# A two-layer diffusion trunk: last norm's statistics on ScalarE, five-operation norm chain, half-step loads reordered, MLP gate rows by TensorE

## The chip, the cores and the metric

The kernel runs on one core of a Trainium2 chip. The metric is the device time of one execution in microseconds (us). Engines are named as the profile names them: PE is TensorE (PEld its weight loads), DVE is VectorE, ACT is ScalarE, POOL is GpSimd, and SP issues every DMA of this kernel, in the order in which they were recorded.

## The reference, cut to what matters

Two transformer-like layers run over 128 context tokens and 512 latent tokens, 1024 wide. Each layer has a mixer and an MLP, and each of these two ends in a layer norm:

```python
def _block(x, mod, mixer, g, b, w1, w2):
    sh1, sc1, gt1, sh2, sc2, gt2 = jnp.split(mod, 6, axis=-1)
    mix, aux = mixer(x * (1 + sc1) + sh1)
    x = _layer_norm(ALPHA * x + gt1 * mix, g[0], b[0])
    hf = x * (1 + sc2) + sh2
    ff = jnp.square(jax.nn.relu(hf @ w1)) @ w2
    x = _layer_norm(ALPHA * x + gt2 * ff, g[1], b[1])
    return x, aux
```

The six rows of `mod` (kinds 0 to 5: shift, scale and gate of the mixer, then of the MLP) come from `silu(cond) @ w_mod[l] + b_mod[l]`, with one condition vector for the context and one for the latents. `w_mod` is 1024 x 6144 for each layer, so it is a matrix product with two rows and 24 MB of weights per layer. Kind 5 is the gate of the MLP. Layer 0's mixer (the even one) is retention beside differential attention; layer 1's (the odd one) is windowed attention beside gated linear attention (GLA). All is float32 in and out.

## The kernel before, in words

The tokens are five tiles of 128 (tile 0 the context). The width is two halves of 512. Every large product is taken in three matmuls of split numbers: a value is cast to a high part (`whi`, `ghi`, `hh`) and the remainder (`wlo`, `glo`, `hl`) is a DVE subtraction; `whi` is an ACT cast. Weights come in units of 512 KB (`wraw`), which are split before PE can use them.

**What sets the order.** All DVE, ACT and POOL operations are recorded by one helper (`Timed.run`, L380), all loads by `load` (L454), matmuls by `mm` (L470), transposes at L485; so most rows of the profile carry these lines, and the tile names tell them apart. A planner (class `Order`, L131) keeps a model of the engines' times while the kernel is being written and interleaves chains of work; the resulting order is fixed. PE executes in that order, and so do the other queues: an engine never passes a waiting instruction.

**The modulation rows** are computed in three ways. The shift and scale of layer 0's mixer are needed at once, and so are computed on PE at the start (`matvec`, in two halves of eight k-steps; tiles `mod` and `wmod`). Kinds 2, 3 and 4 of layer 0 are done by `ModPE` (L634): for each of 6 pieces, two batches of 16 matmuls (`modp<-wmodp,cs`) in the even mixer, a piece every `MOD_PE` = 38 us of the planner's time. Kind 5 of layer 0 and all six of layer 1 are done by `ModChunk` (L574) without PE except for a closing sum over partitions (`modps`): eight steps per chunk of 512 columns, each a 256 KB load, a scaled sum into `moda` for the context column and one for the latent column. In each step with k > 0 POOL does a TENSOR_SCALAR on `wmod` and a TENSOR_TENSOR `moda<-moda,wmod`; the other sum is on ACT (`modp`) and POOL (`moda<-moda,modp`) for layer 0, and one DVE SCALAR_TENSOR_TENSOR (`moda<-wmod,cs,moda`) for layer 1. The `background` function issues a step every `MOD_SPACE` = 3.6 us of planner time from the first MLP on, 14 chunks of 8 steps in all, kind 5 of layer 0 first, and holds them during norms.

**The MLP** has 8 groups g of 512 hidden columns: `ff` (first product), `relu`, square into `ghi` and `glo`, then `fps` (second product). Layer 0's last group is where the next layer's columns are also formed (`A`, `B`).

**The norm** (`norm`, L939) takes, per token tile, two BN_STATS and a BN_AGGR on DVE, a square root on ACT, and six DVE operations on 128x1: `ve`, reciprocal `r`, `q`, `q`, `r`, `nmr`. In the last norm, tiles 0 to 2 (and half of tile 3) are scaled by ACT and multiplied and added by POOL (`x<-x,lnrow`), the rest on DVE.

**The start** (from L1098) loads the first half's 8 k-steps of `w_mod`, four weight units and the inputs xT, forms the first half of the first modulation, modulates the five tiles' first half (`modulated`, two ACT and two POOL operations per tile on `h`, then a cast `h0h` and a remainder `h0l` on DVE) and interleaves early products (`early`) with the second half's matrix-vector steps.

Of the kernel before, what the change touches and what calls it, by code (L numbers as in the profile page):

```python
# [9 lines left out]
F32 = mybir.dt.float32  # L10
F32R = mybir.dt.float32r
I32 = mybir.dt.int32
AF = mybir.ActivationFunctionType
# [5 lines left out]
P = 128  # L19
# [3 lines left out]
KT = 8  # L23
# [13 lines left out]
NSPL = 5  # L37
DEC0, DEC = 0.0, 2.0
MOD_SPACE = 3.6
MOD_PE = 38.0  # L40
LO_POOL = 0
DRS = False
UPD = 30.0
WD = 3
WS = 2
# [362 lines left out]
def trunk_kernel(ctx: ExitStack, tc: tile.TileContext, io: dict, layers: int = 2, stop: str = ""):  # L408
# [3 lines left out]
    const = ctx.enter_context(tc.tile_pool(name="const", bufs=1))  # L412
    hpool = ctx.enter_context(tc.tile_pool(name="hpool", bufs=4))
    gpool = ctx.enter_context(tc.tile_pool(name="gpool", bufs=NSLOT))
    mtmp = ctx.enter_context(tc.tile_pool(name="mtmp", bufs=1))
    mraw = ctx.enter_context(tc.tile_pool(name="mraw", bufs=MRAW))
    wraw = ctx.enter_context(tc.tile_pool(name="wraw", bufs=NRAW))
    wspl = ctx.enter_context(tc.tile_pool(name="wspl", bufs=NSPL))
# [7 lines left out]
    def nm(s):  # L426
        uid[0] += 1
        return f"{s}_{uid[0]}"
# [6 lines left out]
    def sm(s, shape):  # L435
        tag = "s" + "x".join(map(str, shape[1:]))
        t = small.tile(shape, F32, tag=tag, name=nm(s))
        order.reuse(tag, NSMALL, t)
        return t
# [134 lines left out]
    class ModChunk:  # L574
# [10 lines left out]
        def step(self, k):  # L585
            raw = self.raw.pop(k)
            if k == KT - 2:
                self.b = slot("brow")
                src = io["b_mod"][self.l, 512 * self.c:512 * self.c + 512].rearrange("(e n) -> e n", e=2)
                for e in range(2):  # L590
                    load(self.b[64 * e:64 * e + 64, :256], src[e].partition_broadcast(64))
            if k == 0:
                self.A = [slot("moda"), slot("moda")]
            a0, a1 = (a[:, :512] for a in self.A)
            if k == 0:
                act.activation(a0, raw, AF.Copy, scale=cs[:, k, 0:1])
                pool.tensor_scalar(a1, raw, cs[:, k, 1:2], 0.0, op0=ALU.mult, op1=ALU.add)
            else:
                if self.l == 0:
                    tmp = mtmp.tile([P, 512], F32, tag="modp", name=nm("modp"))  # L600
                    order.reuse("modp", 1, tmp)
                    act.activation(tmp, raw, AF.Copy, scale=cs[:, k, 0:1])
                    pool.tensor_tensor(a0, a0, tmp, op=ALU.add)
                else:
                    stt(a0, raw, cs[:, k, 0:1], a0, op0=ALU.mult, op1=ALU.add)
                pool.tensor_scalar(raw, raw, cs[:, k, 1:2], 0.0, op0=ALU.mult, op1=ALU.add)
                pool.tensor_tensor(a1, a1, raw, op=ALU.add)
            if k == KT - 1:
                order.spawn(self.finish())
# [93 lines left out]
                add_piece((l, "2", g, n), [Unit(io["w_2"][l, g, n, u], 2, 512) for u in range(2)])  # L703
    pos = [0, 0, 0]
    mod_steps = []
    for l, kinds in ((0, (5,)), (1, range(6))):
        if l < layers:
            for c in kinds:
                for a in range(2):
                    chunk = ModChunk(l, 2 * c + a)  # L710
                    mod_steps += [(chunk, k) for k in range(KT)]
    mod_left = [0.0, len(mod_steps)]
    mod_hold = [False]
    split_hold = [False]

    mod_pe = [ModPE(2 * c + a) for c in (2, 3, 4) for a in range(2)]

    def load_unit():
        units[pos[2]].load()
        pos[2] += 1  # L720

    def split_unit():
        if pos[0] == pos[2]:
            load_unit()
        units[pos[0]].split()
        pos[0] += 1
# [212 lines left out]
    def norm(t, rows, ft, A, B, final, key, xd=None):  # L939

        cuts = [(0, 0, 512), (1, 0, 512)] if t < NT - 1 else [(0, 0, 256), (0, 256, 512), (1, 0, 256), (1, 256, 512)]
        st = sm("bn", [P, 4, 6])[:, :len(cuts), :]
        mv = sm("mv", [P, 2])
        for i, (a, c0, c1) in enumerate(cuts):
            dve.bn_stats(st[:, i, :], X[t][a][:, c0:c1])
        dve.bn_aggr(mv, st)
        if DRS:
            ve = sm("ve", [P, 1])
            dve.tensor_scalar(ve, mv[:, 1:2], EPS, None, op0=ALU.add)
            r = rsqrt(ve, [P, 1])  # L950
        else:
            ve = sm("ve", [P, 1])
            sq = sm("sq", [P, 1])
            act.activation(sq, mv[:, 1:2], AF.Sqrt, bias=eps_t)
            dve.tensor_scalar(ve, mv[:, 1:2], EPS, None, op0=ALU.add)
            r = sm("r", [P, 1])
            q = sm("q", [P, 1])
            dve.reciprocal(r, sq)
            vec_tt(q, r, r, op=ALU.mult)
            stt(q, q, -0.5, ve, op0=ALU.mult, op1=ALU.mult)  # L960
            stt(r, q, 1.5, r, op0=ALU.add, op1=ALU.mult)
        nmr = sm("nmr", [P, 1])
        stt(nmr, mv[:, 0:1], -1.0, r, op0=ALU.mult, op1=ALU.mult)
        if not final:
            xn = X[t]
            for a in range(2):
# [136 lines left out]
    load_unit()  # L1103
    xt = load_x(0)
    load_unit()
    load_unit()
    ps = acc("mod0")
    for k in range(KT):
        matvec(0, k, ps)
    row = mod_row(ps)  # L1110
    split_unit()
    load_unit()
    dls = slot("dl")
    bc_row(dls[:, :256], io["diff_lam"])
    bc_row(sk, io["swa_sink"])
    for k in range(KT):
        load_mod0(1, k)
    xt1 = load_x(1)
    load(cst[:, C_RC:], io["consts"][:, C_RC:])
    mod_cols(0, row)  # L1120
    order.give()
# [2 lines left out]
    split_unit()  # L1124
    for t in range(1, NT):
        modulated(0, xt, t)
    split_unit()
    split_unit()
    lam(dls)
    ps = acc("mod0")  # L1130
    for k in range(KT):
        for t in range(NT):
# [8 lines left out]
    load_unit()  # L1141
    for t in TURN:
        modulated(1, xt1, t)
    start.close()
    order.give()
    order.fifo = False
# [1017 lines left out]
```

## Time and profile before

| what | value |
|---|---|
| median of 3 runs | 1669.2 us (1667.19 to 1670.53) |
| the profiled execution | 1671.51 us, of which the span is 1669.7 us |
| mean granted PE clock | 0.979 of full speed |
| PE busy | 1579.6 us (95%) |
| DVE busy | 1046.0 us (63%) |
| ACT busy | 619.9 us (37%) |
| POOL busy | 582.2 us (35%) |
| DMA | 177.87 MB, mean 107 GB/s |

PE is busy for 95% of the span, so the kernel's time is PE's work plus the 90 us in which PE is idle or ends before the rest. Where PE waits, the trace names the instruction on another engine that released it. A time at the start of a row counts from the start of the span.

### The profile page before, as it was taken

The page shows a single profiled execution, that of the slowest core. Times are in us where ns is not written, and L with a number is a line of the kernel's source. Part 1 is how long each engine was busy: PE and PEld are TensorE (multiplying, and loading weights), DVE is VectorE, ACT ScalarE, POOL GpSimd, SP SyncE. Part 2 cuts the span into 40 slices and gives each one's busy share as a digit, 9 for nine tenths or more (in the row PEclk, how much of TensorE's full clock was granted, in tenths as well). Part 3 has the DMA queues.
Part 4 walks back from the last instruction along what each step waited for, and adds up shares of the span by engine and source line. Part 5 has one row for each costly group of instructions (what it writes and reads, how often), then busy time and mean ns, then how long its engine had stood idle before and what let it go on. Part 6 is the DMA issues. An engine that isn't in the chain of part 4 may idle for free. (4 is left out here: it accounts for less than half of the span.)

```text
span 1669.7 us, 28365 instructions
## 1 busy us (share of the span) xinstructions
PE 1579.6 (95%) x11233; PEld 1431.6 (86%) x11233; DVE 1046.0 (63%) x1963; ACT 619.9 (37%) x1294; POOL 582.2 (35%) x493
## 2 busy tenths in 40 slices
PE   7999999999999999999898898979999999999995
PEld 4998999998989988998787887869989989998994
DVE  3777762685377667767877787777833334444458
ACT  2555443336433312221265454553543222222221
POOL 1110000111896687678557445340200110011215
PEclk9999999999999999999998998989999999999998
DMA  9523333332444444543424210014222221223121
GB/s 345 185 86 93 97 112 105 130 115 64 137 148 151 146 146 152 171 148 106 146 80 137 73 36 28 27 56 141 76 72 68 76 89 60 72 79 115 55 76 63
DMA packets 89764, 177.87 MB, mean 107 GB/s; under 512 B 23576, under 2 KB 30752, under 8 KB 89632
## 3 DMA queue, kind: packets, MB, share of 16 engines
q1 hardware_dynamic: 89632, 176.07, 32.6%
q8 instruction: 88, 1.44, 0.3%
q14 instruction: 44, 0.36, 0.1%
HBM read 169.53 MB, written 6.50 MB: 105 GB/s over the span
## 5 line engine op out<-in xcount | busy, mean ns | idle before, releaser
L470 PE MATMUL ff<-hh,whi 128*128 128x320 f32 (+2 forms) x960 | 297.1, 309 | 0.0
L470 PE MATMUL ff<-hh,wlo 128*128 128x320 f32 (+2 forms) x960 | 296.4, 309 | 0.1
L470 PE MATMUL ff<-hl,whi 128*128 128x320 f32 (+2 forms) x960 | 296.3, 309 | 0.0
L380 DVE TENSOR_TENSOR wlo<-wraw,whi 128x1024 fp32r<-128x1024 f32 (+1 forms) x183 | 243.3, 1334 | 80.4 <-ACT whi L380 80.2
L380 ACT CAST whi<-wraw 128x1024 fp32r<-128x1024 f32 (+1 forms) x183 | 189.5, 1045 | 278.8 <-PE fps L470 244.7
L470 PE MATMUL fps<-whi,glo 128*128 128x512 f32 (+1 forms) x648 | 254.3, 393 | 5.1 <-DVE glo L380 5.1
L470 PE MATMUL fps<-wlo,ghi 128*128 128x512 f32 (+1 forms) x648 | 253.7, 391 | 2.3 <-DVE wlo L380 2.3
L470 PE MATMUL fps<-whi,ghi 128*128 128x512 f32 (+1 forms) x648 | 254.9, 393 | 0.0
L380 POOL TENSOR_TENSOR x<-x,lnrow 128x512 f32<-128x512 f32 (+1 forms) x76 | 105.9, 1402 | 351.6 <-DVE y L380 214.5
L380 DVE TENSOR_TENSOR relu<-relu 128x320 f32<-128x320 f32 (+3 forms) x100 | 70.7, 707 | 186.6 <-ACT ghi L380 185.6
L470 PEld LDWEIGHTS ff<-hh,whi 128*128 128x128 f32 x960 | 180.2, 188 | 3.1 <-issue 2.1
L470 PEld LDWEIGHTS ff<-hl,whi 128*128 128x128 f32 x960 | 180.2, 188 | 0.6
L470 PEld LDWEIGHTS ff<-hh,wlo 128*128 128x128 f32 x960 | 180.2, 188 | 0.3 <-DVE wlo L380 0.3
L380 ACT ACTIVATE relu<-ff 128x320 f32<-128x320 f32 (+3 forms) x100 | 51.4, 514 | 278.7 <-PE ff L470 276.2
L380 DVE TENSOR_TENSOR y<-fps,y 128x512 f32<-128x512 f32 x120 | 82.7, 689 | 111.6 <-PE fps L470 111.5
L470 PEld LDWEIGHTS fps<-whi,glo 128*128 128x128 f32 x648 | 122.1, 188 | 33.2 <-DVE glo L380 5.5
L380 POOL TENSOR_TENSOR moda<-moda,wmod 128x512 f32<-128x512 f32 x98 | 146.0, 1490 | 6.8
L470 PEld LDWEIGHTS fps<-wlo,ghi 128*128 128x128 f32 x648 | 122.1, 188 | 30.3 <-DVE wlo L380 3.5
L470 PEld LDWEIGHTS fps<-whi,ghi 128*128 128x128 f32 x648 | 122.0, 188 | 29.0 <-issue 2.5
L380 POOL TENSOR_SCALAR wmod<-wmod,cs 128x512 f32<-128x512 f32 x98 | 112.7, 1150 | 92.8 <-DVE moda L380 81.4
L380 POOL TENSOR_TENSOR o<-o,sg 128x640 f32<-128x640 f32 x8 | 13.0, 1621 | 257.7 <-ACT o L380 257.3
L470 PE MATMUL proj<-whi,hh 128*128 128x256 f32 (+1 forms) x280 | 85.1, 304 | 12.5 <-DVE gm L380 7.6
(298 smaller groups left out, 3527.7 us busy)
## 6 DMA issues: line engine op xcount, KB each, us to landing
wraw<-in_w SPq DMA_DIRECT2D x128, 512.0 KB
wmod<-in_w_mod SPq DMA_DIRECT2D x144, 256.0 KB
wraw<-in_w_even SPq DMA_DIRECT2D x24, 512.0 KB
wmodp<-in_w_mod SPq DMA_DIRECT2D x48, 256.0 KB
wraw<-in_w_out SPq DMA_DIRECT2D x16, 512.0 KB
wraw<-in_w_odd SPq DMA_DIRECT2D x16, 512.0 KB
gate<-mrow SPq DMA_DIRECT2D x16, 256.0 KB
xT<-in_xT SPq DMA_DIRECT2D x8, 320.0 KB
```

Source lines behind the costliest of these rows:

```text
L380: i = f(*a, **k)
L470: nc.tensor.matmul(o, a, b, **kw)
```

## The change

Five edits are made together.

1. In the last norm, for tiles 0 to 2, mean and variance come from ACT: two Identity passes with an accumulator (sums, into `part`), a DVE TENSOR_SCALAR for `nmean`, two Square passes with the bias `nmean`, and two DVE TENSOR_SCALARs for `mv`. BN_STATS and BN_AGGR go there.
2. The small chain of all norms has five DVE operations (`veh`, reciprocal in place, `q`, `r`, `nmr`), four of them TENSOR_SCALARs with per-partition operands; before it was six, of which one was TENSOR_TENSOR and three SCALAR_TENSOR_TENSOR.
3. At the start, the third weight unit of four stays where it was, the fourth and the row of `diff_lam` are loaded after the second half's `w_mod` and xT. The two last unit splits move behind the second half's first modulated tile, and `lam` behind all of them.
4. Kind 5 of layer 0 leaves `ModChunk` (16 of 112 steps) and becomes two more pieces of `ModPE` (eight in all).
5. `MOD_PE` is 30 instead of 38.

```diff
-MOD_PE = 38.0
+MOD_PE = 30.0
...
             else:
-                if self.l == 0:
-                    tmp = mtmp.tile([P, 512], F32, tag="modp", name=nm("modp"))
-                    order.reuse("modp", 1, tmp)
-                    act.activation(tmp, raw, AF.Copy, scale=cs[:, k, 0:1])
-                    pool.tensor_tensor(a0, a0, tmp, op=ALU.add)
-                else:
-                    stt(a0, raw, cs[:, k, 0:1], a0, op0=ALU.mult, op1=ALU.add)
+                stt(a0, raw, cs[:, k, 0:1], a0, op0=ALU.mult, op1=ALU.add)
...
-    for l, kinds in ((0, (5,)), (1, range(6))):
-        if l < layers:
-            for c in kinds:
-                for a in range(2):
-                    chunk = ModChunk(l, 2 * c + a)
-                    mod_steps += [(chunk, k) for k in range(KT)]
+    for c in range(6 if layers > 1 else 0):
+        for a in range(2):
+            chunk = ModChunk(1, 2 * c + a)
+            mod_steps += [(chunk, k) for k in range(KT)]
...
-    mod_pe = [ModPE(2 * c + a) for c in (2, 3, 4) for a in range(2)]
+    mod_pe = [ModPE(2 * c + a) for c in (2, 3, 4, 5) for a in range(2)]
...
+        if final and t < 3:
+            junk = slot("junk")[:, :512]
+            part = sm("part", [P, 4])
+            nmean = sm("nmean", [P, 1])
+            for a in range(2):
+                act.activation(junk, X[t][a][:, :512], AF.Identity, accum_out=part[:, a:a + 1])
+            dve.tensor_scalar(nmean, part[:, 0:1], part[:, 1:2], -1.0 / D, op0=ALU.add, op1=ALU.mult)
+            for a in range(2):
+                act.activation(junk, X[t][a][:, :512], AF.Square, bias=nmean, accum_out=part[:, 2 + a:3 + a])
+            dve.tensor_scalar(mv[:, 1:2], part[:, 2:3], part[:, 3:4], 1.0 / D, op0=ALU.add, op1=ALU.mult)
+            dve.tensor_scalar(mv[:, 0:1], nmean, -1.0, None, op0=ALU.mult)
...
+        act.activation(sq, mv[:, 1:2], AF.Sqrt, bias=eps_t)
+        dve.tensor_scalar(veh, mv[:, 1:2], EPS, -0.5, op0=ALU.add, op1=ALU.mult)
+        dve.reciprocal(sq, sq)
+        dve.tensor_scalar(q, sq, sq, veh, op0=ALU.mult, op1=ALU.mult)
+        dve.tensor_scalar(r, q, 1.5, sq, op0=ALU.add, op1=ALU.mult)
+        dve.tensor_scalar(nmr, mv[:, 0:1], -1.0, r, op0=ALU.mult, op1=ALU.mult)
...
     load_unit()
     xt = load_x(0)
     load_unit()
-    load_unit()
...
     split_unit()
+    for k in range(KT):
+        load_mod0(1, k)
+    xt1 = load_x(1)
+    load_unit()
     load_unit()
     dls = slot("dl")
...
-    for k in range(KT):
-        load_mod0(1, k)
-    xt1 = load_x(1)
...
-    split_unit()
-    split_unit()
-    lam(dls)
     ps = acc("mod0")
...
     for t in TURN:
         modulated(1, xt1, t)
+        if t == TURN[0]:
+            split_unit()
+            split_unit()
+    lam(dls)
```

The order on the engines changes with this in places that the diff does not show. On DVE, at the end of layer 0's MLP (last group), before: `relu` and `glo` are the first product's results on their way to the second product, and the `moda` rows are modulation steps of layer 1.

```order
L380 TENSOR_TENSOR glo_8757<-relu_1489_8893,ghi_8756 128x640
L380 SCALAR_TENSOR_TENSOR moda_8798<-wmod_8864,cs,moda_8798 128x512
L380 TENSOR_TENSOR wlo_8934<-wraw_8728,whi_8933 128x1024
L380 TENSOR_TENSOR relu_1492_8928<-relu_1492_8928 128x320
L380 TENSOR_TENSOR glo_8759<-relu_1492_8928,ghi_8758 128x320
L380 SCALAR_TENSOR_TENSOR moda_8798<-wmod_8898,cs,moda_8798 128x512
L380 TENSOR_TENSOR brow_8732<-modps_8972,brow_8732 128x256
L380 TENSOR_TENSOR wlo_8983<-wraw_8836,whi_8982 128x1024
L380 TENSOR_TENSOR relu_1497_8967<-relu_1497_8967 128x320
L380 TENSOR_TENSOR glo_8759<-relu_1497_8967,ghi_8758 128x320
L380 SCALAR_TENSOR_TENSOR moda_8798<-wmod_8937,cs,moda_8798 128x512
```

And now, at the same place of DVE's order:

```order
L379 TENSOR_TENSOR glo_8840<-relu_1492_8963,ghi_8839 128x640
L379 TENSOR_TENSOR wlo_8999<-wraw_8813,whi_8998 128x1024
L379 TENSOR_TENSOR relu_1494_8993<-relu_1494_8993 128x320
L379 TENSOR_TENSOR glo_8842<-relu_1494_8993,ghi_8841 128x320
L379 TENSOR_TENSOR brow_8815<-modps_9032,brow_8815 128x256
L379 TENSOR_TENSOR wlo_9041<-wraw_8911,whi_9040 128x1024
L379 TENSOR_TENSOR relu_1498_9027<-relu_1498_9027 128x320
L379 TENSOR_TENSOR glo_8842<-relu_1498_9027,ghi_8841 128x320
```

All 96 remaining steps now stand 16 steps earlier among the other work, so the last of them has left DVE before these rows. On POOL, in the odd mixer, before: `x<-x,lnrow` rebuilds the trunk's tiles after the MLP's norm, and `gA` and `Eq` belong to the GLA gates.

```order
L380 TENSOR_SCALAR wmod_9910<-wmod_9910,cs 128x512
L380 TENSOR_TENSOR x_4473<-x_4473,lnrow_9062 128x512
L380 TENSOR_TENSOR moda_9907<-moda_9907,wmod_9910 128x512
L380 TENSOR_TENSOR x_4473<-x_4473,lnrow_9066 128x512
L380 TENSOR_SCALAR wmod_10003<-wmod_10003,cs 128x512
L380 TENSOR_SCALAR wmod_10035<-wmod_10035,cs 128x512
L380 TENSOR_TENSOR moda_9907<-moda_9907,wmod_10003 128x512
L380 MEMSET gA_10166 128x5
L380 TENSOR_TENSOR moda_9907<-moda_9907,wmod_10035 128x512
L380 MEMSET gA_10174 128x5
L380 TENSOR_TENSOR Eq_10192<-gA_9955 128x5x64
```

And now, up to the same `Eq`:

```order
L379 TENSOR_TENSOR x_4546<-x_4546,lnrow_9110 128x512
L379 MEMSET gA_9966 128x5
L379 MEMSET gA_9974 128x5
L379 TENSOR_TENSOR x_4546<-x_4546,lnrow_9114 128x512
L379 TENSOR_TENSOR x_4401<-x_4401,lnrow_9108 128x512
L379 TENSOR_TENSOR x_4401<-x_4401,lnrow_9112 128x512
L379 TENSOR_TENSOR x_4589<-x_4589,lnrow_9110 128x512
L379 TENSOR_TENSOR x_4589<-x_4589,lnrow_9114 128x512
L379 TENSOR_TENSOR Eq_10137<-gA_9974 128x5x64
```

No modulation step is left on POOL or DVE in the odd mixer. The last place is DVE in the last norm, before, for tile 2 and the beginning of tile 3 (`fps` is the MLP's second product, `tmp` its product with the gate):

```order
L380 BN_STATS bn_17227<-x_12915 128x6
L380 TENSOR_TENSOR tmp_17224<-fps_17211,gate_16343 128x512
L380 BN_STATS bn_17227<-x_13109 128x6
L380 TENSOR_TENSOR x_12953<-x_12953,tmp_17224 128x512
L380 BN_AGGR mv_17228<-bn_17227 128x2
L380 TENSOR_SCALAR ve_17232<-mv_17228 128x1
L380 TENSOR_TENSOR tmp_17265<-fps_17252,gate_16345 128x512
L380 RECIPROCAL r_17236<-sq_17233 128x1
L380 TENSOR_TENSOR x_13141<-x_13141,tmp_17265 128x512
L380 TENSOR_TENSOR q_17237<-r_17236 128x1
L380 SCALAR_TENSOR_TENSOR q_17237<-q_17237,ve_17232 128x1
L380 SCALAR_TENSOR_TENSOR r_17236<-q_17237,r_17236 128x1
```

And now, for the same stretch:

```order
L379 TENSOR_TENSOR tmp_17202<-fps_17189,gate_16311 128x512
L379 TENSOR_TENSOR x_12933<-x_12933,tmp_17202 128x512
L379 TENSOR_SCALAR nmean_17208<-part_17207 128x1
L379 TENSOR_TENSOR tmp_17248<-fps_17235,gate_16313 128x512
L379 TENSOR_TENSOR x_13114<-x_13114,tmp_17248 128x512
L379 TENSOR_SCALAR mv_17205<-part_17207 128x1
L379 TENSOR_SCALAR mv_17205<-nmean_17208 128x1
L379 TENSOR_SCALAR veh_17216<-mv_17205 128x1
L379 RECIPROCAL sq_17217<-sq_17217 128x1
L379 TENSOR_SCALAR q_17218<-sq_17217,veh_17216 128x1
L379 TENSOR_SCALAR r_17219<-q_17218,sq_17217 128x1
```

Two BN_STATS are gone per tile, and three 128x1 operations wait there for ACT's passes: `nmean` stands ahead of the next tile's second `tmp`, `mv` behind it.

## Rows read from the trace of the kernel before

**Rows 1.** Windows: length, PE, PEld, DVE, ACT, POOL busy, PEclk, DMA share, GB/s.
```profile
27.70:45.00 17.30, 16.73 (x143) 11.51 (x144) 5.07 (x13) 1.62 (x3) 0.71 (x1) 1.00 1.01 376
70.00:345.00 275.00, 266.39 (x2432) 255.86 (x2432) 177.39 (x524) 119.95 (x317) 11.42 (x7) 0.99 0.34 107
345.00:800.00 455.00, 451.08 (x2664) 405.27 (x2663) 307.22 (x387) 154.28 (x248) 308.65 (x234) 1.00 0.42 132
900.00:945.00 45.00, 32.85 (x282) 30.75 (x281) 39.03 (x62) 15.02 (x27) 29.99 (x32) 0.81 0.30 98
1020.00:1121.00 101.00, 81.64 (x842) 71.04 (x840) 75.63 (x196) 50.45 (x139) 46.77 (x55) 0.86 0.11 35
```

**Rows 2.** Timeline of PE, layer 0's last MLP group, then layer 1's; brackets: idle before.
```profile
811.96 0.39 PE L470 MATMUL fps<-whi,ghi 128*128 128x512 f32 x1
...
819.74 0.79 PE L470 MATMUL fps<-whi,glo 128*128 128x512 f32 x1 [5.07 <-DVE glo L380]
...
824.80 0.50 PE L470 MATMUL fps<-wlo,ghi 128*128 128x512 f32 x1 [1.28 <-DVE wlo L380]
...
1621.95 0.39 PE L470 MATMUL fps<-whi,ghi 128*128 128x512 f32 x1
...
1627.53 0.50 PE L470 MATMUL fps<-wlo,ghi 128*128 128x512 f32 x1 [1.01 <-DVE wlo L380]
```

**Rows 3.** Timeline of DVE, in the first of these waits.
```profile
812.08 1.78 DVE L380 SCALAR_TENSOR_TENSOR moda<-wmod,cs,moda 128x512 f32<-128x512 f32 x1
...
814.11 1.61 DVE L380 TENSOR_TENSOR wlo<-wraw,whi 128x1024 fp32r<-128x1024 f32 x1
```

**Rows 4.** Timeline of PE in the odd mixer.
```profile
903.05 2.42 PE L470 MATMUL z<-glT,w 32*128 32x320 f32 x8
913.11 0.58 PE L470 MATMUL proj<-whi,hh 128*128 128x256 f32 x1 [7.64 <-DVE gm L380]
```

**Rows 5.** Timeline of DVE there: the scans of the GLA gates, two groups.
```profile
902.62 8.19 DVE L380 TENSOR_TENSOR_SCAN gA<-ones,ge 128x128 f32<-128x128 f32 x8
...
930.66 1.68 DVE L380 TENSOR_TENSOR_SCAN gA<-ones,ge 128x128 f32<-128x128 f32 x5
```

**Rows 6.** What PE waited for from 895 to 945: total, times, longest.
```profile
PE gl L470 <- DVE gST L380: 2.9, 1, 2.9
PE proj L470 <- DVE ropea L380: 1.6, 1, 1.6
```

**Rows 7.** Groups of instructions: forms, count, busy us, mean ns; layer 0's rows on PE.
```profile
L470 PE MATMUL modp<-wmodp,cs 128*32 128x128 f32 x384 | 13.0, 276 | 0.0
...
L470 PE MATMUL modps<-moda,ones 128*32 128x256 f32 x112 | 8.9, 391 | 0.0
```

**Rows 8.** Timeline of the start, on PE and DVE.
```profile
27.68 0.63 PE L470 MATMUL mod<-wmod,cs 128*32 128x256 f32 x4 [1.74 <-DMA wmod<-in_w_mod]
...
47.73 0.43 DVE L380 CAST h0h<-h 128x512 fp32r<-128x512 f32 x1 [0.36 <-POOL h L380]
...
49.30 0.48 DVE L380 CAST h0h<-h 128x512 fp32r<-128x512 f32 x1 [0.36 <-POOL h L380]
```

**Rows 9.** Timeline of the last norm on DVE and ACT.
```profile
1642.32 1.24 DVE L380 TENSOR_TENSOR q<-r 128x1 f32<-128x1 f32 x1
...
1643.98 0.16 DVE L380 SCALAR_TENSOR_TENSOR nmr<-mv,r 128x1 f32<-128x1 f32 x1
...
1651.26 0.16 DVE L380 SCALAR_TENSOR_TENSOR nmr<-mv,r 128x1 f32<-128x1 f32 x1
...
1644.18 1.52 ACT L380 ACTIVATE x<-x,nmr,r 128x512 f32<-128x512 f32 x2 [4.29 <-DVE nmr L380]
```

**Rows 10.** Groups: accumulating ACT passes, and a small DVE operation of the norms.
```profile
L380 ACT ACTIVATE sp<-ss,smx 128x512 f32<-128x512 f32 x16 | 10.9, 682 | 16.7 <-DVE smx L380 16.3 <-DVE ssum L380 0.4
...
L380 ACT ACTIVATION_READ_ACCUMULATOR sp<-ss,smx 128x1 f32 x40 | 7.9, 198 | 0.0
...
L380 DVE TENSOR_SCALAR ve<-mv 128x1 f32<-128x1 f32 x20 | 3.0, 149 | 0.2
```

More of the change, by code (lines that the diff above doesn't have):

```diff
@@ L39 @@
 MOD_SPACE = 3.6
-MOD_PE = 38.0
+MOD_PE = 30.0
 LO_POOL = 0
-DRS = False
 UPD = 30.0
@@ L414, in trunk_kernel @@
     gpool = ctx.enter_context(tc.tile_pool(name="gpool", bufs=NSLOT))
-    mtmp = ctx.enter_context(tc.tile_pool(name="mtmp", bufs=1))
     mraw = ctx.enter_context(tc.tile_pool(name="mraw", bufs=MRAW))
@@ L941, in norm @@
         cuts = [(0, 0, 512), (1, 0, 512)] if t < NT - 1 else [(0, 0, 256), (0, 256, 512), (1, 0, 256), (1, 256, 512)]
-        st = sm("bn", [P, 4, 6])[:, :len(cuts), :]
         mv = sm("mv", [P, 2])
[L944 to L950, printed above, removed]
-        else:
[L952 to L961, printed above, removed]
@@ L962, in norm @@
-        nmr = sm("nmr", [P, 1])
-        stt(nmr, mv[:, 0:1], -1.0, r, op0=ALU.mult, op1=ALU.mult)
+        if final and t < 3:
[9 more added lines that the diff above has]
+            dve.tensor_scalar(mv[:, 0:1], nmean, -1.0, None, op0=ALU.mult)
+        else:
+            st = sm("bn", [P, 4, 6])[:, :len(cuts), :]
+            for i, (a, c0, c1) in enumerate(cuts):
+                dve.bn_stats(st[:, i, :], X[t][a][:, c0:c1])
+            dve.bn_aggr(mv, st)
@@ L964, in norm @@
+        veh, sq, q, r, nmr = (sm(n, [P, 1]) for n in ("veh", "sq", "q", "r", "nmr"))
+        act.activation(sq, mv[:, 1:2], AF.Sqrt, bias=eps_t)
[4 more added lines that the diff above has]
+        dve.tensor_scalar(nmr, mv[:, 0:1], -1.0, r, op0=ALU.mult, op1=ALU.mult)
         if not final:
```

## The prediction, as put on record before the run

> **What bounds the kernel now.** I read first the busy shares by window, then PE's idle gaps and their releasers in each stretch where PE is not full, and last the other engines in those gaps. PE is the bound almost everywhere: in the even mixer it is busy for 266.4 of 275 us, in layer 0's MLP for 451.1 of 455 [rows 1]. There only PE's own work counts, and DVE or ACT work is free as long as it isn't late. PE is not full in four places. (A) In the last group of layer 0's MLP it waits 5.07 us for `glo`, then 1.28 for `wlo` [rows 2]; DVE spends that time on a modulation step of 1.78 us and a `wlo` of 1.61 [rows 3]. (B) and (C) In the odd mixer, from 900 to 945, PE is busy for 32.85 of 45 us at a mean granted clock of 0.81 [rows 1]: it waits 7.64 us for `gm` [rows 4], 2.9 for `gST` and 1.6 for `ropea` [rows 6]. At the end of that mixer, 1020 to 1121, it is busy for 81.6 of 101 us [rows 1]; the change moves nothing there. The last place is the norm after PE's last product, where DVE's chain sets the end.
>
> The sum is made against the profiled execution, 1671.5 us, which lies 2.3 us above the median of the runs, 1669.2; I apply the difference to the median. A measurement of this kernel can't tell less than about 0.2%, 3.3 us, from no change.
>
> **The start.** The fourth weight unit (512 KB) and `diff_lam`'s row (128 KB), 0.64 MB, go behind the second half's loads. From 27.7 to 45 the DMAs run at 376 GB/s with a busy share of 1.01 [rows 1], so the loads that PE waits for come 0.64 MB / 376 GB/s = 1.7 us earlier. Against it, the split of the last two units now stands behind the second half's first tile: a tile takes 49.30 - 47.73 = 1.57 us on DVE [rows 8], and PE's next early products need these splits, so they may come up to two tile-times later than if split under the DMA's wait. I take a loss of 1.4 and a net of -0.3, range -1.7 (the splits hide) to +1.5 (the gain is eaten by a wait of two tiles).
>
> **Kind 5 on PE.** All batches of ModPE have 16 matmuls, and six pieces are 12 batches: 13.0 us, so 1.08 per batch [rows 7]. Two more pieces add four batches, 4.3 us. Of the partition sums, 8 of 56 go: 8.9 x 8/56 = 1.3 us [rows 7]. Net +3.1, at full price, because PE is full in the even mixer; lower end 0, if the batches fill the 8.6 us that PE idles there, upper end +4.5, if the sums that go were already hidden. A shorter spacing (30 for 38) adds no instruction. The 1 MB per piece is small beside the DMA's share of 0.34 there.
>
> **Place A.** The 96 steps of layer 1 start 16 steps earlier, so none stands beside the last group any more; DVE was busy for only 307 of 455 us in the MLP [rows 1], and takes them there. What A is worth is read from layer 1's MLP, where the same stretch of matmuls runs with no step beside it: 1627.53 - 1621.95 = 5.58 us, against 824.80 - 811.96 = 12.84 in layer 0 [rows 2]. So -7.3; range -5 (the wait of 5.07 alone) to -8.
>
> The mechanism behind it is that DVE and POOL hold each other up: eight `gA` scans take 8.19 us beside POOL's steps, five take 1.68 when POOL is idle [rows 5], that is 1.02 against 0.34 each. The Trainium skill says in "SBUF — State Buffer", section "SBUF: two separate sides", that a DVE operation with two SBUF inputs, or one in a 2-port mode, and a GpSimd operation exclude each other for a whole instruction; on the scans these rows agree with it. It speaks against one part of this change: by that rule the TENSOR_SCALARs of the new small chain would be held as the old operations were, if they count as 2-port ones, and the last norm would gain 1 us less, a sum of -17.2. The trace's `ve` TENSOR_SCALAR is 0.149 us on average of 20 [rows 10], with POOL busy beside many of them, so I don't follow it there.
>
> **Places B and C.** No step stands on DVE or POOL in the odd mixer now, so `gm` follows `z` without the scans' 8.19 us being stretched (at 0.34 they would be 2.7), and POOL's `Eq` no longer stands behind steps. Idle time of PE there is 45 - 32.85 = 12.15 us [rows 1]. The clock takes more: 0.81 over the stretch costs at most 32.85 x 0.19 = 6.2 us, an estimate that counts idle time too; I take 5. That is 17.2 us. What is late next: PE, no longer held, comes earlier to the matmuls that need the gates' chain (z, `gm`, `ge`, scan, `Eq`, `gST`), which keeps its own length. I leave one wait of the kind of C in place, 2.9 + 1.6 = 4.5 us [rows 6]. So -12.7; range -17.2 (all goes) to 0 (PE finds the same waits elsewhere).
>
> **The small chain.** One 128x1 operation of 0.15 us [rows 10] fewer in 20 tiles, and one of `q` that was held 1.24 us in the last norm [rows 9] is now a TENSOR_SCALAR. In the three norms before the last, only the last tile's is on the way to PE: -0.5, range -2 to 0.
>
> **The last norm.** Per tile, DVE loses two BN_STATS and a held `q`, but three operations wait for ACT. ACT's passes are nearest to `sp`, 0.68 + 0.20 = 0.88 us each [rows 10]; four are 3.5, the scaling of the tile 1.5 [rows 9], and with the root, the small operations between (some eight at 0.15 to 0.2) and hand-overs I come to 7.0 to 7.4 us per tile in a ring ACT - DVE - ACT. Before, the tiles' `nmr` are 1651.26 - 1643.98 = 7.28 apart [rows 9]. So tile 3 begins as late as before; after it, two held small operations fall away, each about 1.1, and half of that is hidden. I take -0.5; range -3 (ACT's passes at 0.6) to +3 (at 1.1).
>
> **The sum.** -0.3 + 3.1 - 7.3 - 12.7 - 0.5 - 0.5 = -18.2 us. On the profiled execution 1653.3, on the median 1651.0. I forecast 1651. The terms' ends, not all at once, give 1643 to 1660.
>
> **Rivals.** (1) B and C are given back: PE reaches the end of the odd mixer earlier, but there it waits 101 - 81.6 = 19.4 us on chains of DVE and ACT [rows 1], which start from projections and from the gates; if they are bound by DVE's total work and not by PE, the 12.7 us turn up as waits there. For it: DVE is busy for 75.6 of those 101 us. Against it: these chains' DVE work stands behind the stretched scans on the same queue, so it comes earlier by as much as PE does. Time: 1651 + 12.7 = 1664.
>
> (2) The slower side: SP's one queue. Each ModPE batch's four loads need free buffers from the common pool of 44; 16 batches now do, instead of 12, closer together, and weight units stand behind them in SP's order. If a load blocks there until an even-mixer chain releases a buffer, the units behind are late and PE waits. A late load cost PE 1.74 us in the start [rows 8]; with that price in each of 16 batches it is 27.8 us, and 1651 + 27.8 = 1679. It decides from 18.2 / 16 = 1.1 us per batch. Against it: the even mixer's 8.6 us of idle PE time show that 12 batches are hidden now.
>
> (3) ACT sets the last norm. With passes at 1.1 and the three tiles' rings not overlapped with PE's product the end comes 3 us later instead of 0.5 earlier: 1654.5. The Trainium skill's "ScalarE: Activation LUTs", section "Rules for kernel authors", says that adds and products belong on VectorE and not on ScalarE, which speaks for it; no row before shows Square or a summing Identity.
>
> (4) The steps leave DVE but A and B stay, as the planner's order of `glo` behind `wlo`, or the clock, was their cause. Then only +3.1 and small terms are left: 1671.
>
> **Chances.** Forecast 0.70, (1) 0.13, (2) 0.06, (3) 0.07, (4) 0.04. Faster by over 0.2% (below 1665.9): the forecast, (3), and most of (1): 0.88. Within 0.2%: the rest of (1) and most of (4): 0.06. Slower (above 1672.5): (2): 0.06. The forecast's own range is 1643 to 1660; reaching to (1) gives 1643 to 1664.
>
> **What would show it.** A: the stretch from the first `fps` of layer 0's last group to the matmul that waited for `wlo` is about 5.6 us, and no `moda` stands in DVE's rows after it. B: `gA` scans near 0.34 us, PE's gap before `proj` after `z` under 3 us, mean granted clock 900 to 945 above 0.9. PE's `modp` group 17.3 us. Last norm: `nmr` of tiles 7.0 to 7.4 apart, ACT passes 0.9. The prediction is wrong if the odd mixer's waits stay above 8 us in that stretch, if weight waits appear in the even mixer, or if its last 100 us grow by as much as B and C lose.

## The result and the profile after

The changed kernel takes 1647.8 us (median of 4 runs, 1645.1 to 1651.3), against 1668.9 for the kernel before on the same chip: a ratio of 0.9875, 95% interval 0.9854 to 0.9896, some 21 us. The forecast was 1651, range 1643 to 1664 (1643 to 1660 without its first rival). Time and direction came out, but two terms of the sum were far off, in opposite directions, and the experiments below show both.

To see where the 24 us between the two profiled spans (1669.7 and 1645.8) came from, read the same landmarks in each trace: the first or last start of a group of matmuls. `sd` is the first product of the even mixer's attention, `ff` the MLP's first product (read at the first `ff<-hh,whi`; some `ff` on other weights start 10.3 us earlier in both kernels), `z` the GLA gates' first product in the odd mixer, `ops` the mixers' output product, `fps` the MLP's second product.

| stretch, us | before | after | difference | forecast |
|---|---|---|---|---|
| start to first `sd` | 69.3 | 74.4 | +5.1 | -0.3 |
| first `sd` to first `ff` (even mixer) | 317.4 | 320.4 | +3.0 | +4.3 |
| first `ff` to first `z` (MLP and A) | 498.9 | 493.2 | -5.7 | -8.6 |
| first `z` to last `ops` (odd mixer) | 309.7 | 283.4 | -26.3 | -12.7 |
| last `ops` to last `fps` (MLP) | 455.6 | 456.4 | +0.8 | 0 |
| last `fps` to the end | 18.8 | 18.0 | -0.8 | -0.5 |

(The forecast's +3.1 for kind 5 is split here into +4.3 in the even mixer and -1.3 in the MLP; its -0.5 for the small chain in earlier norms is left out.)

The windows of the changed kernel that answer to [rows 1]: length, then PE, PEld, DVE, ACT, POOL busy, the granted clock, the DMA share, GB/s.

```profile
70.00:345.00 275.00, 265.22 (x2540) 252.66 (x2530) 176.26 (x526) 120.68 (x321) 11.26 (x7) 0.99 0.38 120
345.00:800.00 455.00, 451.11 (x2676) 405.20 (x2675) 312.37 (x400) 145.31 (x234) 278.74 (x215) 1.00 0.44 135
900.00:945.00 45.00, 43.75 (x428) 41.29 (x427) 35.48 (x80) 24.66 (x55) 11.73 (x19) 0.96 0.22 72
1020.00:1121.00 101.00, 90.14 (x892) 78.60 (x892) 76.87 (x221) 54.33 (x149) 36.85 (x44) 0.93 0.17 54
```

From 900 to 945 PE is idle for 1.25 us instead of 12.15, at a mean granted clock of 0.96 instead of 0.81. The stretch from 1020 to 1121, which the forecast left alone, has lost 8.5 us of idle time too. Place A is gone; the timeline of PE, from the first `fps` of the last group to the matmul that waited for `wlo`:

```profile
820.48 0.39 PE L468 MATMUL fps<-whi,ghi 128*128 128x512 f32 x1
...
826.06 0.50 PE L468 MATMUL fps<-wlo,ghi 128*128 128x512 f32 x1 [1.01 <-DVE wlo L379]
```

That is 5.58 us, which is what layer 1 took in [rows 2], and 7.3 less than before. All that PE waited for from 895 to 945, and the GLA scans of that stretch on DVE (against [rows 6] and [rows 5]):

```profile
PE sqT L483 <- DVE qq L379: 0.8, 1, 0.8
PE gl L468 <- DVE Ek L379: 0.4, 1, 0.4
```

```profile
921.35 3.26 DVE L379 TENSOR_TENSOR_SCAN gA<-ones,ge 128x128 f32<-128x128 f32 x10
```

Ten scans take 3.26 us, 0.33 each, as the unheld ones did before. The start is where time was lost. PE, then ACT and DVE:

```profile
56.40 0.39 PE L468 MATMUL early<-whi,h0h 128*128 128x256 f32 x1 [3.64 <-ACT v L379]
```

```profile
54.60 0.20 ACT L379 ACTIVATE ls<-ls 128x2 f32<-128x2 f32 x1 [5.27 <-DVE ls L379]
54.71 0.35 ACT L379 COPY qk<-early 128x256 f32<-128x256 f32 x1
54.96 1.05 ACT L379 CAST whi<-wraw 128x1024 fp32r<-128x1024 f32 x1
55.91 0.43 ACT L379 COPY v<-early 128x128 f32<-128x128 f32 x2
```

```profile
53.36 0.69 DVE L379 TENSOR_TENSOR h0l<-h,h0h 128x512 fp32r<-128x512 f32 x1
53.97 0.28 DVE L379 TENSOR_TENSOR dl<-dl 128x128 f32<-128x128 f32 x1
54.28 0.29 DVE L379 TENSOR_REDUCE ls<-dl 128x2 f32<-128x128 f32 x1
```

Read them from the back. `lam` stands behind the last `h0l` on DVE. Its exponential stands in ACT's queue ahead of the copies of `qk` and `v`, whose source PE had finished by 52.8 us at the latest; ACT sits idle 5.27 us for 0.20 us of work, and PE, which needs the bank that the copy of `v` empties, waits 3.64. The earlier loads did help: the second half's modulation row is transposed at 42.7 us instead of 44.3.

On PE the groups that answer to [rows 7], and in the last norm the rows that answer to [rows 9] and [rows 10], on DVE and ACT:

```profile
L468 PE MATMUL modp<-wmodp,cs 128*32 128x128 f32 x512 | 17.7, 281 | 0.0
...
L468 PE MATMUL modps<-moda,ones 128*32 128x256 f32 x96 | 7.7, 391 | 0.0
```

```profile
1613.79 0.21 DVE L379 TENSOR_SCALAR nmr<-mv,r 128x1 f32<-128x1 f32 x1
...
1620.98 0.21 DVE L379 TENSOR_SCALAR nmr<-mv,r 128x1 f32<-128x1 f32 x1
...
1627.96 0.21 DVE L379 TENSOR_SCALAR nmr<-mv,r 128x1 f32<-128x1 f32 x1
...
1633.92 0.26 DVE L379 TENSOR_SCALAR q<-sq,veh 128x1 f32<-128x1 f32 x1
```

```profile
1617.22 0.73 ACT L379 ACTIVATE junk<-x,nmean 128x512 f32<-128x512 f32 x1 [0.28 <-DVE nmean L379]
1617.85 0.19 ACT L379 ACTIVATION_READ_ACCUMULATOR junk<-x,nmean 128x1 f32 x1
```

The tiles' `nmr` are 7.19 and 6.98 us apart, as forecast (7.0 to 7.4), and no `q` is held: all 20 take 0.26 to 0.27 us.

### The profile page after: what moved, and what is told of

It reads as the page before. It is cut to its first block, busy times and chain, and to the rows that moved or that the text cites. A ratio compares the mean times of both kernels' runs of the same rounds, so it can differ in the third digit from the quotient of the medians.

```text
span 1645.8 us, 28545 instructions
## 1 busy us (share of the span) xinstructions
PE 1573.2 (96%) x11345; PEld 1425.2 (87%) x11345; DVE 1019.2 (62%) x1945; ACT 619.1 (38%) x1302; POOL 523.6 (32%) x449
## 4 chain that ended last, share of the span: by engine, by line
PE 82%; DVE 7%; ACT 4%; POOL 3%; issue 2%; DMA 2%; SPq 0%; POOLq 0%; DVEq 0%; ACTq 0%
PE ff L468 25%; PE fps L468 24%; PE proj L468 12%; PE ops L468 6%; PE fproj L468 3%; ACT h L379 1%; PE sd L468 1%; PE early L468 1%; PE odp L468 1%; PE po L468 1%; DMA wmod<-in_w_mod 1%; POOL y L379 1%; PE modp L468 1%; DVE wlo L379 1%; DVE x L379 1%
## 5 line engine op out<-in xcount | busy, mean ns | idle before, releaser
L379 DVE TENSOR_TENSOR wlo<-wraw,whi 128x1024 fp32r<-128x1024 f32 (+1 forms) x183 | 243.4, 1335 | 74.4 <-ACT whi L379 74.1
L379 DVE TENSOR_TENSOR relu<-relu 128x320 f32<-128x320 f32 (+3 forms) x100 | 65.1, 651 | 188.2 <-ACT ghi L379 187.2
L379 POOL TENSOR_SCALAR wmod<-wmod,cs 128x512 f32<-128x512 f32 x84 | 95.6, 1138 | 125.0 <-DVE moda L379 109.4
L379 POOL TENSOR_TENSOR moda<-moda,wmod 128x512 f32<-128x512 f32 x84 | 123.7, 1472 | 6.3
L468 PE MATMUL proj<-whi,h0h 128*128 128x256 f32 x320 | 92.0, 287 | 0.9 <-DVE catl L379 0.5
```

The source lines that it names most:

```text
L379: i = f(*a, **k)
L468: nc.tensor.matmul(o, a, b, **kw)
```

## The experiments

Theory after the result: the steps' time on DVE and POOL, not their place in the planner's order, made the stalls in the MLP and the odd mixer; edit 4 holds the whole gain; the start's edits lose time. Each kernel was timed beside the kernel before on its chip, whose median there was 1671.3 us (e1 to e4), 1669.8 (e5 to e8) and 1671.7 (e9 to e12).

| run | what it is | median us | ratio to before, 95% |
|---|---|---|---|
| e9_again | the changed kernel once more | 1647.0 | 0.9858 (0.9836 to 0.9880) |
| e1_ghost16 | before, 14 steps without their time (kind 5 of layer 1 is left out of the result) | 1646.8 | 0.9865 (0.9848 to 0.9881) |
| e7_ghost_pool | the same for POOL alone | 1653.5 | 0.9901 (0.9885 to 0.9917) |
| e8_space32 | before, steps 3.2 apart | 1649.5 | 0.9872 (0.9856 to 0.9889) |
| e2_k5pe38 | before + kind 5 on PE | 1644.6 | 0.9844 (0.9829 to 0.9859) |
| e12_k5pe30 | the same, spacing 30 | 1638.5 | 0.9799 (0.9778 to 0.9821) |
| e3_start_old | after, start as before | 1638.2 | 0.9805 (0.9790 to 0.9820) |
| e4_lam_early | after, `lam` as before | 1646.8 | 0.9854 (0.9837 to 0.9870) |
| e10_loads_old | after, loads as before | 1647.0 | 0.9860 (0.9837 to 0.9884) |
| e11_start_mix | after, a third start | 1641.4 | 0.9819 (0.9803 to 0.9836) |
| e5_stat_dve | e3, statistics on DVE | 1637.9 | 0.9806 (0.9792 to 0.9821) |
| e6_chain_old | e3, old small chain | 1636.9 | 0.9801 (0.9786 to 0.9815) |

### Is it the steps' time or the order? (e1, e7)

```diff
             a0, a1 = (a[:, :512] for a in self.A)
+            cut = {"cut": 1} if (self.l, self.c // 2) == (1, 5) else {}
...
-                    stt(a0, raw, cs[:, k, 0:1], a0, op0=ALU.mult, op1=ALU.add)
-                pool.tensor_scalar(raw, raw, cs[:, k, 1:2], 0.0, op0=ALU.mult, op1=ALU.add)
-                pool.tensor_tensor(a1, a1, raw, op=ALU.add)
+                    stt(a0, raw, cs[:, k, 0:1], a0, op0=ALU.mult, op1=ALU.add, **cut)
+                pool.tensor_scalar(raw, raw, cs[:, k, 1:2], 0.0, op0=ALU.mult, op1=ALU.add, **cut)
+                pool.tensor_tensor(a1, a1, raw, op=ALU.add, **cut)
```

The planner still counts 512 columns, so PE, DVE, ACT and POOL keep the order of before, and only the execution of these operations is short. e7 leaves `cut` off the first of the three.

> The kernel before, in its own order on every engine; the 14 steps (k > 0) of layer 1's kind 5, those that stand at the end of the MLP and in the odd mixer, work on one column instead of 512, so that kind's rows are left out of the result, and only the time of these steps goes. Theory (the steps' time on DVE and POOL made the stalls): place A's stretch falls from 12.8 to about 5.6 us and the odd mixer loses 17 to 25 us, so 1640 to 1648 us in all. Rival (the gain of the changed kernel's odd mixer came from the planner's new order of PE): only A and the wait for gm shrink, about 7 and 5 us, and the time is 1655 to 1660 us.

> As e1_ghost16 (the kernel before in its own order, layer 1's kind 5 partly left out), but only POOL's two operations of the 14 steps work on one column; DVE's moda keeps its 512. Theory (POOL's operations stretch DVE's): most of e1's gain stays, 1650 to 1656 us. Rival (it was DVE's own 14 operations of about 1 us in its queue): less than half stays, 1660 us or more.

The whole odd mixer, from first `z` to last `ops`, as one window: the kernel before, then e1, e7 and the changed kernel.

```profile
885.60:1195.30 309.70, 275.64 (x2667) 250.24 (x2667) 241.07 (x523) 145.08 (x357) 133.27 (x145) 0.93 0.21 70
```

```profile
877.30:1169.20 291.90, 269.38 (x2667) 244.23 (x2667) 226.77 (x522) 144.75 (x357) 118.12 (x145) 0.96 0.22 74
```

```profile
878.90:1174.40 295.50, 271.62 (x2667) 246.49 (x2667) 231.41 (x522) 145.05 (x357) 118.44 (x145) 0.95 0.22 73
```

```profile
888.00:1171.40 283.40, 265.61 (x2650) 241.12 (x2650) 217.79 (x508) 144.32 (x356) 103.64 (x121) 0.97 0.21 69
```

With the order untouched and the steps' time gone, 309.7 us become 291.9: 17.8 us less, of which 11.5 are idle time of PE and 6.3 its busy time, at a mean granted clock of 0.96 instead of 0.93. Place A goes too, in e1 as in the changed kernel:

```profile
810.45 0.39 PE L472 MATMUL fps<-whi,ghi 128*128 128x512 f32 x1
...
816.04 0.50 PE L472 MATMUL fps<-wlo,ghi 128*128 128x512 f32 x1 [1.01 <-DVE wlo L382]
```

This is the theory, and the rival (order) is wrong for this part. The rest up to the changed kernel's 283.4, 8.5 us, comes with all else that the change does there: the planner's new order above all, and the 16 matmuls of `modps` and the one-column remains of the steps that e1 still has in the mixer. It was not taken apart further. What e1 still waits for in the odd mixer (total, times, longest):

```profile
PE spT L487 <- DVE sg L382: 4.5, 2, 2.9
PE proj L472 <- DVE ropea L382: 3.8, 2, 3.2
PE U L472 <- ACT pT L382: 3.5, 1, 3.5
PE ss L472 <- DVE smx L382: 2.8, 1, 2.8
PE gkwT L487 <- DVE sg L382: 2.6, 1, 2.6
```

`gm` is down to 0.4 and `gST` off the list; the other waits are close to those of before (4.7, 4.9 with the 1.6 of place C, 3.5, 2.8 and 2.6 us there). They belong to the old order, and the planner, which has no steps to place there now, interleaves other work: in the changed kernel's list over the same stretch `ropea`, `smx` and the wait for `pT` by `U` are missing, and a 5.7 for `sg` and a 3.0 for `catl` are new.

One part of the new order can be named. The ten `gA` scans, of which [rows 5] shows eight, stood beside more than steps: for 4.0 of the 8.2 us POOL was at `x<-x,lnrow`, which no step needs. In e1 the ten still take 5.42 us. In the changed kernel POOL is done with these operations at 894.8, ahead of the first scan at 900.3, and all 20 scans take 0.33 to 0.34. POOL before, then DVE in e1:

```profile
903.80 2.65 POOL L380 TENSOR_TENSOR x<-x,lnrow 128x512 f32<-128x512 f32 x2
```

```profile
890.43 5.42 DVE L382 TENSOR_TENSOR_SCAN gA<-ones,ge 128x128 f32<-128x128 f32 x10
```

e7 keeps 16 of e1's 24 us (1669.8 - 1653.5 against 1671.3 - 1646.8), as the theory expected. By the totals two thirds of the stalls go with POOL's operations. By the landmarks it is more: place A goes whole (PE waits 1.1 us there), and the odd mixer is 295.5 us, so that 14.2 of the 17.8 stay. That POOL stretches DVE's operations is seen in the ten scans, which take 10.31 us before, 6.46 in e7 and 5.42 in e1; what POOL's own queue adds, in which `Eq` stood behind steps, was not separated, and no run takes out DVE's `moda` alone.

### Steps out of the odd mixer without PE (e8)

```diff
-MOD_SPACE = 3.6
+MOD_SPACE = 3.2
```

> The kernel before with one number changed: a modulation step every 3.2 instead of 3.6 us of planner time, so that all 112 steps stand ahead of the MLP's norm and none in the odd mixer; kind 5 of layer 0 stays off PE, the start and the norms are as before. Theory (what matters is only that no step stands in the odd mixer): 1641 to 1648 us. Rival (DVE and POOL are too full in the MLP at this spacing, and PE waits for y or glo there): 1652 us or more.

Between the two expectations. The odd mixer is as short as in the changed kernel (first `z` 891.9, last `ops` 1174.2: 282.3 us), so it does suffice that no step stands there. But first `ff` to first `z` is 503.1 us, against 493.2 in the changed kernel and 498.9 before. DVE and POOL in the MLP, by the same columns as above:

```profile
345.00:800.00 455.00, 448.39 (x2651) 400.64 (x2650) 323.23 (x396) 153.63 (x248) 338.34 (x252) 1.00 0.45 139
```

POOL is busy for 338 us where the changed kernel's is for 279, PE for 2.7 less, and place A isn't quite cleared: PE still waits there for `glo`. So the rival holds in part.

```profile
824.87 0.64 PE L470 MATMUL fps<-whi,glo 128*128 128x512 f32 x1 [2.22 <-DVE glo L380]
```

### Kind 5 on PE alone (e2, e12)

```diff
-    for l, kinds in ((0, (5,)), (1, range(6))):
+    for l, kinds in ((1, range(6)),):
...
-    mod_pe = [ModPE(2 * c + a) for c in (2, 3, 4) for a in range(2)]
+    mod_pe = [ModPE(2 * c + a) for c in (2, 3, 4, 5) for a in range(2)]
```

e12 has `MOD_PE = 30.0` as well.

> The kernel before with kind 5 of layer 0 on TensorE alone, the spacing still 38. Theory: this edit holds the whole gain: A -7, odd mixer -25, even mixer +3, so about 1641 to 1645 us, faster than the changed kernel by what the start costs there (5 us). Rival (the start's edits cost nothing by themselves, and the 5 us lost before 75 us come with the new order): 1646 to 1650 us, as the changed kernel.

> The kernel before with two edits only, kind 5 of layer 0 on TensorE and the spacing 30. Theory (statistics and small chain are worth nothing, as e5_stat_dve and e6_chain_old say): the same as e3_start_old, 1636 to 1640 us. Rival (the two norm edits hide each other's worth): 1641 us or more.

e2 is in the theory's range, at its upper end; e12 is the theory exactly: two edits of the five hold all of the gain and more, 33 us against 25 for all five on the same chip. The spacing is worth 6 us, and they are lost around the MLP's start: the first `fps` comes at 415.8 us in e2 and at 409.3 in e12. From the first `ff<-hh,whi` to it are 31.3 us in e2 and 23.9 in e12, but part of that is order, since the first `ff` of all is at 378.7 and 375.1. That stretch in e2, then in e12:

```profile
384.50:415.80 31.30, 27.86 (x162) 26.99 (x161) 14.42 (x28) 15.90 (x36) 6.16 (x4) 0.89 0.16 51
```

```profile
385.40:409.30 23.90, 23.33 (x147) 22.63 (x145) 10.37 (x18) 11.79 (x27) 0.60 (x1) 1.00 0.19 66
```

With pieces 38 apart the last `modp` matmuls come at 358.8 us, in the midst of the mixer's output product, instead of 298.7, ahead of it. In the stretch shown the mean granted clock is 0.89, POOL has 6 us of work, and PE waits 2.8 us for `hh`. Which of these makes the loss was not taken apart.

What do the four added batches cost? In e12 `modp` takes 17.3 us on PE, 4.3 more than before as forecast, yet the first `ff` is at 385.4 us, before at 386.7. The window of the even mixer in e12:

```profile
70.00:345.00 275.00, 269.05 (x2570) 257.65 (x2570) 177.56 (x530) 121.56 (x319) 11.32 (x7) 1.00 0.40 125
```

PE is busy for 2.7 us more than in [rows 1]: part of the batches fill what was idle. The cost is 0, the lower end of my bound, but only with the spacing of 30: in e2 the first `fps` is 5.2 us later than before (410.6).

### What the start costs (e3, e4, e9, e10, e11)

e3 undoes the start's part of the diff as a whole. e4 puts back the load of `diff_lam` (the small row of `sink` goes with it) and `lam` alone; the lines of the loads are left out here:

```diff
     for t in range(1, NT):
         modulated(0, xt, t)
+    lam(dls)
     ps = acc("mod0")
...
             split_unit()
             split_unit()
-    lam(dls)
```

e10 puts back the loads' order alone, and e11 is a third way:

```diff
     for t in range(1, NT):
         modulated(0, xt, t)
+    split_unit()
...
         if t == TURN[0]:
             split_unit()
-            split_unit()
-    lam(dls)
     start.close()
     order.give()
     order.fifo = False
+    lam(dls)
```

> The changed kernel with the start's loads, splits and lam as before. Theory: the first sd matmul comes at 69.3 us again instead of 74.4, and the time is 1643 us (1647.8 - 5.1). Rival (the planner hides the delay in the even mixer's slack): 1647 us or more.

> The changed kernel with diff_lam's load and lam alone put back ahead of the second half; the fourth unit and the two splits stay where the change put them. Theory (lam's Exp waits in ACT's queue ahead of the copies of v, for which PE waits 3.6 us): the wait goes, 1643 to 1645 us. Rival (the splits behind the first tile cost it): 1647 us or more.

> The changed kernel itself, beside the next three on one chip. If the start's edits cost about 10 us, as e3_start_old against the changed kernel says, 1646 to 1650 us here; if that was a difference between chips, 1638 to 1641.

> The changed kernel with the start's loads in the order of before; the last two unit splits and lam stay behind the second half's tiles. Theory (splits and lam behind the tiles cost the start its time, and the loads' own gain is 1.6 us): 1648 to 1651 us. Rival (the fourth unit's late arrival makes the loss): 1638 to 1640 us.

> The changed kernel with the third unit split ahead of the second half, the fourth behind its first tile, and lam behind the whole start; the loads as the change has them. Theory (the loads' gain stays and nothing in ACT's queue holds the copies of v): the first sd near 69 us, 1636 to 1640 us. Rival (any other start sends the planner into a longer even mixer, whose first ff was 8 us late in the changed kernel): 1642 us or more with the first sd near 69 us.

The changed kernel again took 1647.0, so it isn't the chip. e3 took 1638.2 and not the 1643 expected: the start's edits cost 9 us, more than the 5 that I read from the first `sd`. With the old start (e3) the first `sd` is at 69.6 us and the first `ff` at 386.2; with the new one at 74.4 and 394.8 (73.3 and 392.2 in the second profile). So 4 to 5 us are lost before `sd` and 2 to 4 more in the even mixer; the rest is too small to be placed.

e4 takes out most of the wait for `v`,

```profile
57.45 0.39 PE L468 MATMUL early<-whi,h0h 128*128 128x256 f32 x1 [0.85 <-ACT v L379]
```

and its first `sd` is at 71.0, 3.4 us earlier than in the changed kernel. So `lam` did hold the copies. But its total is 1646.8, which is the rival's number (the splits) and not the theory's: the first `ff` is at 394.3. The even mixer, 323.3 us long, gives the 3.4 us back. The theory was right on the place and wrong on the total. In the changed kernel, in e4 and in e10 PE waits there for `qkh`, 3.1 us in one wait that neither the kernel before nor e3 nor e11 has; the changed kernel's:

```profile
160.37 0.64 PE L468 MATMUL sd<-qkh,qkh 128*128 128x320 f32 x1 [3.13 <-DVE qkh L379]
```

The planner times the whole mixer from its start, and orders PE otherwise after another start.

e10, with the old loads but the late splits and `lam`, is as slow as the changed kernel, 1647.0, just below the theory's range: the late fourth unit is not to blame. e11 is 3 us slower than e3. That was neither side's number (1636 to 1640, or 1642 and up), nearer to the rival: its first `ff` is at 386.8, no earlier than e3's, and in its profile 4 us more go in small parts behind it.

The starts side by side, from single profiles: when PE transposes the second half's modulation row, when the first `sd` comes, and the median of the runs.

| kernel | splits of the last two units | `lam` | row, us | first `sd`, us | between | median us |
|---|---|---|---|---|---|---|
| e3 | ahead of the second half | ahead | 44.5 | 69.6 | 25.1 | 1638.2 |
| e11 | one ahead, one behind its first tile | last | 42.2 | 68.1 | 25.9 | 1641.4 |
| e4 | both behind its first tile | ahead | 43.7 | 71.0 | 27.3 | 1646.8 |
| changed | both behind its first tile | late | 42.7 | 74.4 | 31.7 | 1647.8 |
| e9, the same | both behind its first tile | late | 41.7 | 73.3 | 31.6 | 1647.0 |
| e10 | both behind its first tile | late | 45.4 | 77.0 | 31.6 | 1647.0 |

In the stretch between, the late `lam` costs 4.3 us (e4 against the changed kernel) and the late splits 2.2 (e3 against e4, which has the fourth unit later too). The totals go another way. They don't follow `lam` or the loads, but the splits: 1647 with both late, 1641 with one, 1638 with none. How much of that is the splits' own lateness and how much the other order of PE that the planner then chooses isn't shown, and no run moves the splits alone.

### The norms (e5, e6)

e5 is e3 with `if final and t < 0`, e6 is e3 with the six operations of before in `norm`.

> The kernel of e3_start_old with the last norm's statistics of tiles 0 to 2 on DVE again (BN_STATS), all else as there. Theory (the ring over ACT takes as long per tile as DVE's own chain did): within 1.5 us of e3_start_old, 1637 to 1640 us. Rival (moving the statistics is what shortened the tail): 3 us or more slower, 1641 us and up.

> The kernel of e3_start_old with the six-operation chain of the kernel before in all norms. Theory (two or three held 128x1 operations of 1.1 us in the last norm, and little elsewhere): 1 to 3 us slower, 1639 to 1641 us. Rival (the new TENSOR_SCALARs cost as much as they save, since they take 0.21 to 0.27 us each instead of 0.15): no difference, 1638 us.

Neither makes a difference that the runs can tell: 1637.9 and 1636.9 against e3's 1638.2. For the statistics that is the theory; for the small chain it is the rival. The traces show more. From the last `fps` to the end it is 18.8 us before, 18.9 in e6 (ACT's statistics, old chain), 18.8 in e12 (DVE's, old chain), 17.4 in e3 (both new), and 15.4 in e5 (DVE's statistics, new chain). In e5 the next tile's `nmr` comes 5.17 us after the last:

```profile
1614.10 0.21 DVE L379 TENSOR_SCALAR nmr<-mv,r 128x1 f32<-128x1 f32 x1
...
1619.27 0.21 DVE L379 TENSOR_SCALAR nmr<-mv,r 128x1 f32<-128x1 f32 x1
```

So the small chain shortens the tail by 3.4 us where the statistics stay on DVE, and moving the statistics to ACT gives 2 of them back. It's a reading of single profiles (the tail with both new is 17.4 to 18.1 us in the six that have it), and against the scatter of the totals (e5's own runs go from 1636.5 to 1639.1) it is not shown in the times.

No run beats the old start with edit 4 and the spacing: e12, e3, e5 and e6 lie within 1.7 us of one another, 32 to 33 us below the kernel before and about 9 below the changed kernel.

## Why the prediction was right, and where it was not

- **Place A**, -7.3: right, to the tenth (5.58 us for the stretch). The reading by layer 1's MLP held. The MLP as a whole gained 5.7 instead of 8.6; the 1.3 of `modps` did not show, and the rest is not settled.
- **B and C**, -12.7: the mechanism was right, the size not; the odd mixer lost 26.3 us. Two steps failed. I left one wait of 4.5 us in place as "what is late next"; e1 shows that with the steps gone and the order kept, 17.8 us go, which is the 17.2 that I had counted before that deduction (11.5 idle and 6.3 by the clock, where I had 12.15 and 5). And I held that "the change moves nothing" at the end of the mixer: another 8.5 us come with the new order, part of them there. The scans' 8.19 us, which I put down to POOL's steps, were for about half beside `x<-x,lnrow`. PE's order of instructions in that stretch, compared before and after, could have shown that something moves there.
- **Kind 5 on PE**, +3.1 "at full price, because PE is full": the price of the batches was right (17.7 us for `modp`), the claim that nothing hides it was not. PE had 8.6 us of idle time in that stretch, and in e12 the batches cost nothing. The shorter spacing, which I put at nothing because it "adds no instruction", is what makes it so: it is worth 6 us (e2 against e12). A piece loads 2 MB, not 1 (48 loads of 256 KB for six pieces in the kernel before), which changed nothing.
- **The start**, -0.3 with +1.5 as the upper end: this step failed most. The gain of the loads was right (1.6 us by the transpose of the modulation row, 2.6 in e9's profile). I weighed the two splits at a loss of 1.4 us and passed over `lam`, which the same lines of the diff move, and ACT's queue behind it: e4 and the rows above show 3.4 us there. But the start's edits cost 9 us in all (e3), and that loss goes with the splits, not with `lam`: e4 has `lam` back and gains nothing. I had counted only what the splits hold up at once, and not that the planner orders the mixer behind them anew; no row of before could price that.
- **The last norm and the small chain**, -0.5 and -0.5: right in size (-0.8 from last product to end), the ring over ACT as forecast; but by the profiles the small size is two larger effects, -3.4 and +2, that nearly cancel, which I had not seen. On ACT four passes of 0.8 to 0.9 us stand against two BN_STATS of 0.68 on DVE, and the tail is 2 us shorter in e5's profile, with no difference in the medians. The Trainium skill's "ScalarE: Activation LUTs", section "Rules for kernel authors", prefers VectorE for adds and products; the profiles agree with it, the times don't decide. The new `q` takes 0.26 us at 1633.92, beside a busy POOL, and isn't held, as I took it, though my reason was weaker than I wrote: POOL was busy beside 6 of the 20 `ve`, not many. The Trainium skill's "SBUF — State Buffer", section "SBUF: two separate sides", would have it held if it counted as a 2-port operation; the trace shows no sign of that.
- **Rivals.** (1), the gain given back at the end of the mixer: no, those waits are in e1 what they were before. (2), weight units late behind ModPE's loads: PE waits for no weight load in the even mixer, and for `wlo` 1.1 us as before. (3), ACT sets the tail: by 2 us in the traces, not seen in the totals. (4): no.

That the total came out is in part luck: a loss of some 9 us by the start's edits where I had a gain of 0.3, and 13.6 us more gain in the odd mixer, partly cancelled. Had I priced `lam` alone correctly, the forecast would have been farther off.

## What to carry to other kernels

A stall made by background work is best priced at a place where the same code runs without it; the twin gave A exactly, and leaving the work's time out in its own order (e1) gave 17.8 of the odd mixer's 26.3 us. Price every instruction that a moved line takes along, small ones above all, by what stands behind it in its engine's queue: 0.2 us of `lam` held a copy for which PE waited 3.6. But a wait that goes is not yet time that goes: without it (e4) the total stayed at 1647. When a planner sets the order, try each edit alone on the chip: two of these five edits made 33 us, one lost 9, and two made none that the runs can tell.

## What the runs showed that I had not expected

- Background work off the bound engine is not free: 14 steps of 0.99 us on DVE and of 1.15 + 1.49 us on POOL (means over all steps before) made 24.5 us of the kernel's time (e1), 1.75 for each, two thirds or more by POOL's part. That is more than a step's time on DVE and less than its time on POOL.
- A TENSOR_SCALAR on 128x1 with per-partition operands takes 0.20 to 0.27 us, where the SCALAR_TENSOR_TENSOR on the same shape took 0.16 [rows 9]; it gains only where the other was held.
- A start that is no slower at its end (e11, first `sd` at 68.1; the kernels with the old start have it at 68.3 to 69.7) ends 3 us later than e3.
